# Low part of the MLP weights: an accumulating DMA in place of a VectorE subtraction

## The chip, the cores and the metric

The kernel runs on one core of one Trainium2 chip, and the other cores have no part in it. The metric is the device time of one execution in microseconds. A change is told from no change when the times differ by more than about 2%.

## The reference

One decoder layer in float32 on 512 tokens of 1024 channels: a combined input projection, a recurrent branch and an attention branch, their merge and output projection, then the MLP and a gated per-layer embedding. The change touches the weights of the MLP line alone:

```python
x += (sigmoid(gate_a) * A + sigmoid(gate_b) * B) @ w_out
x += relu(RMSNorm(x) @ w_up)^2 @ w_down          # w_up 1024x4096, w_down 4096x1024
x += (p[l] @ w_ple_proj) * sigmoid(RMSNorm(x) @ w_ple_gate)
```

## The kernel before

All weights lie packed in HBM as 144 units of [128, 1024] float32 (512 KB each), and `weight_order` lists them in order of use. Float32 products are made of three fp32r products: a factor is split into a high part (rounded to fp32r) and a low part (what the rounding left), and `mm3` adds high x high, high x low and low x high. One unit feeds 8 such triples, 24 matmuls of 512 columns, by `proj`.

A unit goes through three steps in `wsplit`. SyncE's queue (SP) loads it into a raw tile `wr`, of which there are two. ScalarE (ACT) copies it into `wh`, which rounds it. VectorE (DVE) subtracts `wh` from `wr` into `wl`. There are four buffers each of `wh` and `wl`. `wload(u)` hands out unit u and first issues the units that follow until four are ready or on their way (`AHEAD = 3`), so the split of unit u+3 is written just ahead of the matmuls of unit u, and it waits until the matmuls of unit u-1 have left their `wh` and `wl`.

The MLP runs in four groups of 1024 hidden channels. A group has 8 up units, each followed by the scaling with `r1`, the squared relu and the split of the result into `us`, and then 8 down units, each of which is added onto `x1`. That makes 64 units, from `U_MLP` = 70 to 133. They follow the 8 units of the output projection (62 to 69), and the per-layer embedding follows them (134 to 143). While the output projection and the last down group run, `sq_accumulate` adds squares on GpSimd (POOL), which has nothing else to do in these stages.

PE, ACT, SP and POOL run their instructions in the order in which the code is written, each engine for itself; a waiting instruction holds up all that stand behind it on its engine. Only VectorE's order is picked by a scheduler.

```python
for c in cuts:
    nc.sync.dma_start(raw[:, c], w_all[u][:, c])
for c in cuts:
    nc.scalar.activation(wh[:, c], raw[:, c], AF.Copy)
    nc.vector.tensor_tensor(out=wl[:, c], in0=raw[:, c], in1=wh[:, c].bitcast(F32),
                            op=ALU.subtract)
```

Of the kernel before, what the change touches and what calls it, by code (L numbers as in the profile page):

```python
# [24 lines left out]

# units of [128, 1024] in the packed weights, in order of use
U_QKV = 0
# [12 lines left out]

# columns of the packed per-channel vectors, 8 each
V_GMIX, V_GMLP, V_GPLE, V_CB, V_BRG, V_BIG, V_LAM, V_CW = 0, 8, 16, 24, 32, 40, 48, 56
N_VEC = 56 + 4 * 8


AHEAD = 3  # weight units split ahead of the one in use
F_BUFS = 24
W_BUFS = 4
N_WARM = 18
CUT = 6  # chunks of a gate projection before the turn of the next queries  # L50
LAG = 2  # chunks between a projection of the recurrent branch and its gates


def weight_order():
    """The units in order of use."""
    def run(u, n=KC):
        return list(range(u, u + n))

    o = run(U_QKV, 12) + run(U_GB) + run(U_GA)
    for m in range(KC + LAG):  # L60
        if m < KC:
            o.append(U_X + m)
        if m >= LAG:
            o.append(U_ATT + m - LAG)
    o += run(U_G) + run(U_RNN) + run(U_OUT) + run(U_MLP, 64) + run(U_PLE, 2) + run(U_PG)
    assert sorted(o + run(U_GATE, 2)) == list(range(N_UNITS))
    return o
# [3 lines left out]
def layer_kernel(ctx, tc, w_all, x_t, p_t, vecs, row, ctab, out_t):  # L71
# [5 lines left out]
    ps = ctx.enter_context(tc.tile_pool(name="ps", bufs=1, space=PSUM))  # L77
    # these engines run their instructions in the order in which they are written here
    E = mybir.EngineType
    ctx.enter_context(tc.manual_schedule(engines={E.PE, E.Activation, E.SP, E.Pool}))  # L80

    def rtile(name):
        """Both parts of four chunks of an activation."""
        return act.tile([P, 4, 2, S], F32R, tag="r", name=name, bufs=4)
# [15 lines left out]

# [1 line left out]
    order = weight_order()  # L102
# [6 lines left out]
    def wsplit(u, pool, bufs, parts=1):  # L109
        raw = wp.tile([P, 1024], F32, tag="wr", name=f"wr{u}", bufs=2)  # L110
        wh = pool.tile([P, 1024], F32R, tag="wh", name=f"wh{u}", bufs=bufs)
        wl = pool.tile([P, 1024], F32R, tag="wl", name=f"wl{u}", bufs=bufs)
        n = 1024 // parts
        cuts = [slice(i * n, (i + 1) * n) for i in range(parts)]
        for c in cuts:
            nc.sync.dma_start(raw[:, c], w_all[u][:, c])
        for c in cuts:
            nc.scalar.activation(wh[:, c], raw[:, c], AF.Copy)  # L118
            nc.vector.tensor_tensor(out=wl[:, c], in0=raw[:, c], in1=wh[:, c].bitcast(F32),  # L119
                                    op=ALU.subtract)  # L120
        return wh, wl

    def wload(u):
        """Unit u, with the units that follow on their way."""
        while u not in ready or (order and len(ready) <= AHEAD):
            wissue()
        return ready.pop(u)

    def split(src, r):
        """r[:, 0] + r[:, 1] = src, both parts exact in 12 bits."""  # L130
        nc.scalar.activation(r[:, 0, :], src, AF.Copy)  # L131
        nc.vector.tensor_tensor(
            out=r[:, 1, :], in0=src, in1=r[:, 0, :].bitcast(F32), op=ALU.subtract
        )

    def split_scaled(src, scale, r):
        """The same for src * scale[partition]."""
        nc.scalar.activation(r[:, 0, :], src, AF.Copy, scale=scale)
        nc.vector.scalar_tensor_tensor(
            out=r[:, 1, :], in0=src, scalar=scale, in1=r[:, 0, :].bitcast(F32),  # L140
            op0=ALU.mult, op1=ALU.subtract,
        )
# [6 lines left out]
    def proj(out, w, acts, ks=range(KC), kcs=KC, w0=0, t=slice(0, S)):  # L149
        """out[c, t] = sum over k of w[k, c] * acts[k, t]."""  # L150
        wh, wl = w
        for k in ks:
            c = slice(w0 + k * P, w0 + (k + 1) * P)
            a = chunk(acts, k)
            mm3(out, wh[:, c], wl[:, c], a[:, 0, t], a[:, 1, t], k == 0, k == kcs - 1)

# [1 line left out]
    vec = const.tile([P, N_VEC], F32, name="vec")  # L158
# [16 lines left out]

# [1 line left out]
    def rms_bcast(sqacc, name):  # L177
        """(mean over channels + eps) ** -0.5 for each token, on every partition."""
        pb = tr_ps(f"pb_{name}")
        nc.tensor.matmul(pb, ones, sqacc, start=True, stop=True)  # L180
        ms = ftile(f"ms_{name}")
        nc.vector.tensor_scalar(out=ms, in0=pb, scalar1=1.0 / D, scalar2=EPS,
                                op0=ALU.mult, op1=ALU.add)
        y = act.tile([P, S], F32, tag="rb", name=f"rb_{name}", bufs=1)
        nc.scalar.activation(y, ms, AF.Abs_reciprocal_sqrt)
        t = ftile(f"nt_{name}")
        nc.vector.tensor_tensor(out=t, in0=y, in1=y, op=ALU.mult)
        nc.vector.tensor_tensor(out=t, in0=t, in1=ms, op=ALU.mult)
        nc.vector.tensor_scalar(out=t, in0=t, scalar1=-0.5, scalar2=1.5,
                                op0=ALU.mult, op1=ALU.add)  # L190
        nc.vector.tensor_tensor(out=y, in0=y, in1=t, op=ALU.mult)
        return y

    def warm_up():
        """Keeps the tensor engine busy, and its clock up, until the first loads are in."""
        pw = tr_ps("pw")
# [8 lines left out]

# [1 line left out]
    xg = rtiles("xg")  # L207
# [13 lines left out]

# [1 line left out]
    att_scope = ExitStack()  # L223
# [4 lines left out]
    def qkv_group(grp, name, after=()):  # L228
        """Projections with tokens on the partitions; after[i]() is emitted behind part i."""
        banks = [mm_ps(f"{name}{n}") for n in range(NB)]  # L230
# [18 lines left out]
    def token_stats():  # L249
        """The mean squares with tokens on the partitions."""  # L250
        ptk = tr_ps("ptk")
# [8 lines left out]

    # rotary tables with the gains folded in: out = t * cc + swap_halves(t) * ss
    def rope_tables(gain, mul, name):
# [21 lines left out]
    def k_side(banks):  # L284
        """Normalized and rotated k of all tokens, v scaled by the norm of its token."""
        kraw = big("kraw")
# [42 lines left out]
    def k_split(kraw, n):  # L329
        # both parts, each doubled, so that a transpose fills all partitions  # L330
        k2 = att.tile([P, 2, 4, 2, HD], F32R, tag="qs", name=f"k2_{n}", bufs=2)
# [29 lines left out]
    def q_scale(u):  # L361
        """(sum of squares over a head + 64 eps mean(x^2)) ** -0.5"""
        n = u % NB
# [144 lines left out]

    # c4 = 4 * softplus(-lambda)
    lam = vec[:, V_LAM : V_LAM + 8]  # L510
# [9 lines left out]
    for d in (15, 13, 11, 9, 7, 5, 3):  # L520
        nc.vector.scalar_tensor_tensor(out=pl, in0=pl, scalar=1.0 / d, in1=s2,
                                       op0=ALU.add, op1=ALU.mult)
    # 4 * log1p(e) = 8 * s * (1 + pl)
    nc.vector.scalar_tensor_tensor(out=pl, in0=pl, scalar=1.0, in1=s_,
# [31 lines left out]

# [1 line left out]
    o = [rtile("o0"), rtile("o1")]  # L558
# [43 lines left out]

# [1 line left out]
    rnn = None  # L604
# [21 lines left out]
    def gate_weights(i):  # L626
        """The gates' weights of two chunks."""
        raw = wp.tile([P, S], F32, tag="wr", name=f"wrg{i}", bufs=2)
# [19 lines left out]
    def gate_post(m, xc, both):  # L648
        r, ig = both
        nc.gpsimd.tensor_tensor(out=ig, in0=ig, in1=xc, op=ALU.mult)  # L650
        # t = tanh(-log_a / 2); a = exp(log_a) = 1 - t (1 + a); sqrt(1 - a^2) = sqrt(t) (1 + a)
        nc.scalar.activation(xc, r, AF.Tanh, scale=cs[:, 0, m : m + 1])
        batch.append((m, r, ig, xc))
# [21 lines left out]
    rnn_scope = ExitStack()  # L675
    later = [[], []]  # what is left of the recurrence, for the next two steps

# [75 lines left out]

# [1 line left out]
    def reload(m):  # L755
# [15 lines left out]

# [1 line left out]
    pr = ple.tile([P, 2, 2, S], F32R, name="pr")  # L773
# [29 lines left out]

# [1 line left out]
    es = []  # L805
# [32 lines left out]

# [1 line left out]
def _units(w):  # L840
    """[1024, 128 n] -> [n, 128, 8 * 128]: unit m holds columns 128 m.., k on the partitions."""
    import numpy as np
# [6 lines left out]
def _pack(i):  # L849
# [30 lines left out]
    row = np.concatenate([i["sinks"][0], i["q_gain"][0], i["k_gain"][0]]).reshape(1, 144)  # L880
    # constants of the shapes: rotary angles and the window's mask
    inv = (10000.0 ** (-np.arange(0, 64, 2) / 64)).astype(np.float32)
# [28 lines left out]
```

## Time and profile before

| | |
|---|---|
| executions timed | 861.26 and 861.58 us, median 861.42 us |
| span of the profiled execution, first to last instruction | 859.3 us |
| PE busy | 851.2 us, 99% of the span |
| DVE busy | 530.6 us, 62% |
| ACT busy | 360.3 us, 42% |
| POOL busy | 113.1 us, 13% |
| granted TensorE clock, mean | 0.999 |

The profiled execution's own time is known by its span: from its first to its last instruction it took 859.3 us, 2.1 us below the median of the timed executions, and these 2.1 us are taken to lie around the first and the last instruction. Busy shares are means over stages with different limits. A matmul's duration in the rows includes its way through the array, and matmuls overlap, so the pace of PE is read from the starts, not from the durations.

### The profile page before, as it was taken

What the parts mean: (1) busy time and instruction counts of PE and PEld (TensorE: products, weight loads), DVE (VectorE), ACT (ScalarE), POOL (GpSimd) and SP (SyncE); (2) the same over time, 40 slices, a digit from 0 to 9 for tenths busy, and PEclk for the clock granted to TensorE, in tenths of its full rate; (3) what the DMA queues carried; (4) which work ended last, traced back from release to release, by engine and by line L of the source; (5) the groups of instructions that cost most, each with busy time, mean ns of one, the idle gap of its engine ahead of it and who ended that gap; (6) DMA issues with size and microseconds to landing.
All of it is one profiled execution on the core that took longest, in us unless ns stands there. A gap on an engine that the chain in (4) does not pass through costs nothing.

```text
span 859.3 us, 10186 instructions
## 1 busy us (share of the span) xinstructions
PE 851.2 (99%) x3922; PEld 698.9 (81%) x3922; DVE 530.6 (62%) x754; ACT 360.3 (42%) x578; POOL 113.1 (13%) x127
## 2 busy tenths in 40 slices
PE   9999999999999999999999999999999999999997
PEld 8878878777788878888888888888888888888886
DVE  4676787778578886776557643564346434655374
ACT  7342656565557787442434221222122212233431
POOL 2811343323111110000120000000000000002100
PEclk9999999999999999999999999999999999999999
DMA  6332212111223222333342332223223222222231
GB/s 238 122 98 74 74 50 74 63 62 50 75 86 110 74 74 94 117 130 127 136 146 84 98 122 93 81 98 102 98 95 98 98 99 98 98 94 93 84 123 50
DMA packets 25536, 83.35 MB, mean 97 GB/s; under 512 B 2960, under 2 KB 3344, under 8 KB 25488
## 3 DMA queue, kind: packets, MB, share of 16 engines
q1 hardware_dynamic: 25344, 82.66, 28.6%
q8 instruction: 31, 0.51, 0.2%
q14 instruction: 17, 0.14, 0.1%
q10 hardware_dynamic: 144, 0.05, 0.0%
HBM read 80.60 MB, written 2.10 MB: 96 GB/s over the span
## 4 chain that ended last, share of the span: by engine, by line
PE 80%; DVE 8%; ACT 6%; DMA 2%; issue 2%; POOL 1%; SPq 0%; ACTq 0%; DVEq 0%; POOLq 0%
PE pu L145 7%; PE pd L147 7%; PE pu L147 7%; PE pd L145 7%; PE pd L146 7%; PE pu L146 7%; PE pgate L145 3%; PE pgate L146 3%; PE pgate L147 3%; DVE xc L619 3%; DVE wl L119 2%; ACT wh L118 2%; PE S L421 2%; PE ppg L147 2%; PE ppg L145 2%; PE ppg L146 2%
## 5 line engine op out<-in xcount | busy, mean ns | idle before, releaser
L119 DVE TENSOR_TENSOR wl<-wr,wh 128x1024 fp32r<-128x1024 f32 (+1 forms) x143 | 179.8, 1258 | 55.9 <-ACT wh L118 55.8
L118 ACT ACTIVATE wh<-wr 128x1024 fp32r<-128x1024 f32 (+1 forms) x143 | 149.0, 1044 | 120.2 <-PE pd L146 96.2
L145 PE MATMUL pu<-x1g,wh 128*128 128x512 f32 x256 | 100.0, 391 | 0.0
L146 PE MATMUL pu<-x1g,wh 128*128 128x512 f32 x256 | 99.6, 389 | 0.0
L147 PE MATMUL pu<-x1g,wl 128*128 128x512 f32 x256 | 99.6, 389 | 0.0
L145 PE MATMUL pd<-u,wh 128*128 128x512 f32 x256 | 99.6, 389 | 0.0
L146 PE MATMUL pd<-u,wh 128*128 128x512 f32 x256 | 99.6, 389 | 0.0
L147 PE MATMUL pd<-u,wl 128*128 128x512 f32 x256 | 99.6, 389 | 0.0
L204 POOL TENSOR_TENSOR sq<-sq,sq_x 128x512 f32<-128x512 f32 x14 | 18.2, 1298 | 456.8 <-ACT sq_x L202 456.8
L131 ACT ACTIVATE u<-up 128x512 fp32r<-128x512 f32 x32 | 20.2, 632 | 126.5 <-DVE up L790 126.5
L799 DVE TENSOR_TENSOR xr<-pd,xr 128x512 f32<-128x512 f32 x32 | 22.1, 692 | 81.4 <-PE pd L147 81.4
L146 PEld LDWEIGHTS pu<-x1g,wh 128*128 128x128 f32 x256 | 48.1, 188 | 10.2 <-issue 0.2
L145 PEld LDWEIGHTS pu<-x1g,wh 128*128 128x128 f32 x256 | 48.1, 188 | 10.1 <-issue 0.2
L147 PEld LDWEIGHTS pu<-x1g,wl 128*128 128x128 f32 x256 | 48.1, 188 | 10.0
L146 PEld LDWEIGHTS pd<-u,wh 128*128 128x128 f32 x256 | 48.1, 188 | 10.0
L147 PEld LDWEIGHTS pd<-u,wl 128*128 128x128 f32 x256 | 48.1, 188 | 10.0
L145 PEld LDWEIGHTS pd<-u,wh 128*128 128x128 f32 x256 | 48.1, 188 | 9.9
L458 POOL TENSOR_SCALAR sm<-sm,st 128x256 f32<-128x256 f32 (+1 forms) x64 | 39.5, 633 | 96.1 <-DVE st L456 57.9
L145 PE MATMUL pgate<-xg,wh 128*128 128x512 f32 x128 | 51.3, 401 | 0.0
L147 PE MATMUL pgate<-xg,wl 128*128 128x512 f32 x128 | 50.1, 391 | 0.0
L146 PE MATMUL pgate<-xg,wh 128*128 128x512 f32 x128 | 50.1, 391 | 0.0
L789 DVE TENSOR_TENSOR up<-pu,rb_x 128x512 f32<-128x512 f32 x32 | 22.1, 691 | 40.0 <-PE pu L147 40.0
(225 smaller groups left out, 1704.6 us busy)
## 6 DMA issues: line engine op xcount, KB each, us to landing
wr<-in_w_all SPq DMA_DIRECT2D x141, 512.0 KB, 3.3
x<-in_x_t SPq DMA_DIRECT2D x8, 256.0 KB, 4.8
xr<-in_x_t SPq DMA_DIRECT2D x8, 256.0 KB, 3.6
out<-pgt SPq DMA_DIRECT2D x7, 256.0 KB, 2.1
wrg<-in_w_all SPq DMA_DIRECT2D x4, 256.0 KB, 2.9
wr<-in_w_all SPq DMA_DIRECT2D x2, 256.0 KB, 3.2
pk<-in_p_t SPq DMA_DIRECT2D x2, 256.0 KB, 3.7
tab<-in_ctab SPq DMA_DIRECT2D x1, 256.0 KB, 6.2
```

The source lines that it names most:

```text
L118: nc.scalar.activation(wh[:, c], raw[:, c], AF.Copy)
L119: nc.vector.tensor_tensor(out=wl[:, c], in0=raw[:, c], in1=wh[:, c].bitcast(F32), op=ALU.subtract)
L131: nc.scalar.activation(r[:, 0, :], src, AF.Copy)
L145: nc.tensor.matmul(out, ah, bh, start=start, stop=False)
L146: nc.tensor.matmul(out, ah, bl, start=False, stop=False)
L147: nc.tensor.matmul(out, al, bh, start=False, stop=stop)
L204: nc.gpsimd.tensor_tensor(out=acc, in0=acc, in1=t, op=ALU.add)
L421: nc.tensor.matmul(pss[:, i, :], q_t[u, g][:, i, :], kt[part][:, kv, b0 * P : b0 * P + 256], start=part == 0, stop=part == 1)
L458: nc.gpsimd.tensor_scalar(out=sm[:, i, :], in0=sm[:, i, :], scalar1=den[:, i : i + 1], scalar2=1.0, op0=ALU.mult, op1=ALU.mult)
L619: nc.vector.scalar_tensor_tensor(out=xc[:, sft:], in0=xb[:, : S - sft], scalar=col(V_CW + 8 * j, m), in1=xc[:, sft:], op0=ALU.mult, op1=AL ...
L789: nc.vector.tensor_tensor(out=y, in0=pu, in1=r1, op=ALU.mult)
L799: nc.vector.tensor_tensor(out=x1[m], in0=pd, in1=x1[m], op=ALU.add)
```

## The change

For the 64 MLP units alone, ACT makes both parts: it copies the raw unit into `wh`, and copies it again with scale -1 into `wl`, which then holds the negated high part. GpSimd's queue then issues a DMA that reads the raw unit and adds it onto `wl` in SBUF, 512 KB onto 512 KB. What is left in `wl` is raw minus high, as before. The subtraction on VectorE is gone for these units. All other units, and the numbers of buffers, stay as they are. The remaining lines of the diff drop comments and shift line numbers by 6.

```diff
         for c in cuts:
             nc.sync.dma_start(raw[:, c], w_all[u][:, c])
+        if U_MLP <= u < U_PLE:
+
+            nc.scalar.activation(wh, raw, AF.Copy)
+            nc.scalar.activation(wl, raw, AF.Copy, scale=-1.0)
+            nc.gpsimd.dma_start(wl, raw, accum_op=ALU.add)
+            return wh, wl
         for c in cuts:
             nc.scalar.activation(wh[:, c], raw[:, c], AF.Copy)
             nc.vector.tensor_tensor(out=wl[:, c], in0=raw[:, c], in1=wh[:, c].bitcast(F32),
```

SP's queue at the turn from the output projection to the MLP, before, with what each instruction waits for (`wr70` is the raw tile of the first MLP unit, `xr` a reloaded chunk of x, `pk` a small input):

```order
L116 DMA wr71_3796<-in_w_all 128x1024 [waits DMAHW0_49,DVE_49]
L757 DMA xr7_3802<-in_x_t 128x512 [waits DMAHW5_49]
L116 DMA wr72_3835<-in_w_all 128x1024 [waits DMAHW2_49,DVE_49]
L776 DMA pk0_3873<-in_p_t 128x512 [waits DMAHW7_49]
L776 DMA pk1_3877<-in_p_t 128x512
L116 DMA wr73_3884<-in_w_all 128x1024 [waits DMAHW4_49,DMAHW1_49,DVE_49]
L116 DMA wr74_3931<-in_w_all 128x1024 [waits DMAHW6_49,DVE_49]
```

The same place of SP's queue with the change (DMASW is the semaphore of a DMA issued by GpSimd):

```order
L116 DMA wr71_3797<-in_w_all 128x1024 [waits DMAHW0_49,DVE_49]
L763 DMA xr7_3804<-in_x_t 128x512 [waits DMAHW5_49]
L116 DMA wr72_3837<-in_w_all 128x1024 [waits DMAHW2_49,DMASW0_49,Activation_49]
L782 DMA pk0_3876<-in_p_t 128x512 [waits DMAHW7_49]
L782 DMA pk1_3880<-in_p_t 128x512
L116 DMA wr73_3887<-in_w_all 128x1024 [waits DMAHW1_49,DMAHW4_49,DMASW1_49,Activation_49]
L116 DMA wr74_3935<-in_w_all 128x1024 [waits DMAHW6_49,DMASW2_49,Activation_49]
```

From unit 72 on, the load into a raw tile waits for the accumulating DMA that read that tile two units earlier, where it waited for VectorE's subtraction; the order itself has not moved.

ACT in the first up group before, where `u0_0` is the split of an up result and `wh74`, `wh75` are high parts:

```order
L131 ACTIVATE u0_0_3882<-up0_0_3926 128x512 [waits DVE_49]
L118 ACTIVATE wh74_3932<-wr74_3931 128x1024 [waits DMAHW2_49,PE_49,Activation_49]
L131 ACTIVATE u0_0_3882<-up0_1_3962 128x512 [waits DVE_49]
L118 ACTIVATE wh75_3968<-wr75_3967 128x1024 [waits DMAHW3_49,PE_49,Activation_49]
L131 ACTIVATE u0_0_3882<-up0_2_3998 128x512 [waits DVE_49]
```

ACT at the same place with the change:

```order
L137 ACTIVATE u0_0_3885<-up0_0_3930 128x512 [waits DVE_49]
L119 ACTIVATE wh74_3936<-wr74_3935 128x1024 [waits DMAHW2_49,PE_49,Activation_49]
L120 ACTIVATE wl74_3937<-wr74_3935 128x1024 [waits DMASW0_49,PE_49]
L137 ACTIVATE u0_0_3885<-up0_1_3967 128x512 [waits DVE_49]
L119 ACTIVATE wh75_3973<-wr75_3972 128x1024 [waits DMAHW3_49,PE_49,Activation_49]
L120 ACTIVATE wl75_3974<-wr75_3972 128x1024 [waits DMASW1_49,PE_49]
L137 ACTIVATE u0_0_3885<-up0_2_4004 128x512 [waits DVE_49]
```

A second copy of 1024 columns stands behind each high part, and it waits for the matmuls and for the accumulating DMA that last used its buffer, four units earlier.

POOL at the turn to the MLP with the change (before, the three `sq1` additions stand in a row, and no DMA is in POOL's queue anywhere):

```order
L121 DMA wl70_3759<-wr70_3757 128x1024 [waits DMAHW2_49,DVE_49,Activation_49]
L210 TENSOR_TENSOR sq1_3563<-sq1_3563,sq_x1_5_3794 128x512 [waits Activation_49,Pool_49]
L121 DMA wl71_3799<-wr71_3797 128x1024 [waits DMAHW4_49,DVE_49,Activation_49]
L210 TENSOR_TENSOR sq1_3563<-sq1_3563,sq_x1_6_3834 128x512 [waits Activation_49,Pool_49]
L121 DMA wl72_3839<-wr72_3837 128x1024 [waits DMAHW6_49,DVE_49,Activation_49]
L210 TENSOR_TENSOR sq1_3563<-sq1_3563,sq_x1_7_3872 128x512 [waits Activation_49,Pool_49]
L121 DMA wl73_3889<-wr73_3887 128x1024 [waits DMAHW1_49,DVE_49,Activation_49]
```

The 64 DMAs are new in POOL's queue, the first few and the last few between additions of squares, the others with nothing between them.

## Rows read from the trace of the kernel before

**Rows 1.** Busy time by stretch: one down group, one up group, the end.

```profile
core 0: us, PE busy (x) PEld busy (x) DVE busy (x) ACT busy (x) POOL busy (x), PEclk, DMA share, GB/s
...
494.00:537.00 43.00, 43.00 (x192) 35.61 (x191) 16.72 (x18) 9.02 (x9) 0.00 (x0) 1.00 0.32 106
537.00:581.00 44.00, 44.00 (x196) 36.45 (x195) 25.02 (x30) 12.14 (x15) 0.00 (x0) 1.00 0.26 88
...
799.00:859.30 60.30, 55.74 (x267) 46.63 (x265) 30.06 (x41) 19.61 (x28) 1.29 (x1) 0.98 0.26 88
```

**Rows 2.** Timeline of PE: first matmul of the MLP and first one behind it.

```profile
449.96 0.39 PE L145 MATMUL pu<-x1g,wh 128*128 128x512 f32 x1
...
799.00 0.39 PE L145 MATMUL pe<-pr,wh 128*128 128x512 f32 x1
```

**Rows 3.** Timeline of ACT in a down group: start, duration, instruction, idle before and releaser.

```profile
592.30 1.06 ACT L118 ACTIVATE wh<-wr 128x1024 fp32r<-128x1024 f32 x1 [4.38 <-PE pd L146]
597.74 1.06 ACT L118 ACTIVATE wh<-wr 128x1024 fp32r<-128x1024 f32 x1 [4.38 <-PE pd L146]
603.13 1.06 ACT L118 ACTIVATE wh<-wr 128x1024 fp32r<-128x1024 f32 x1 [4.33 <-PE pd L146]
```

**Rows 4.** Timeline of DVE and of SP's queue in the same stretch.

```profile
593.39 1.23 DVE L119 TENSOR_TENSOR wl<-wr,wh 128x1024 fp32r<-128x1024 f32 x1 [0.23 <-ACT wh L118]
...
594.65 0.33 SPq L116 DMA_DIRECT2D wr<-in_w_all  x1
```

**Rows 5.** DMA queues and issues: count, KB each, us from issue to landing.

```profile
q1 hardware_dynamic: 25344, 82.66, 28.6%
...
wr<-in_w_all SPq DMA_DIRECT2D x141, 512.0 KB, 3.3
...
out<-pgt SPq DMA_DIRECT2D x7, 256.0 KB, 2.1
...
tab<-in_ctab SPq DMA_DIRECT2D x1, 256.0 KB, 6.2
out<-pgt SPq DMA_DIRECT2D x2, 128.0 KB, 1.7
```

**Rows 6.** Instructions by line and shape from 450 to 800 us: busy us, mean ns, idle before.

```profile
L119 DVE TENSOR_TENSOR wl<-wr,wh 128x1024 fp32r<-128x1024 f32 x64 | 80.2, 1254 | 17.7 <-ACT wh L118 17.7
L118 ACT ACTIVATE wh<-wr 128x1024 fp32r<-128x1024 f32 x64 | 67.3, 1051 | 98.4 <-PE pd L146 96.2 <-issue 2.2
```

**Rows 7.** Waits of SP's queue: total us, times, longest.

```profile
SPq L116 <- DVE wl L119: 562.4, 116, 11.1
```

**Rows 8.** Timeline of POOL at the end of the output projection.

```profile
441.40 1.29 POOL L204 TENSOR_TENSOR sq<-sq,sq_x 128x512 f32<-128x512 f32 x1 [4.15 <-ACT sq_x L202]
446.84 1.29 POOL L204 TENSOR_TENSOR sq<-sq,sq_x 128x512 f32<-128x512 f32 x1 [4.15 <-ACT sq_x L202]
```

## The prediction, made before the run

> **What bounds the kernel now.** I read the busy time by stretch first. The MLP runs from the first `pu` matmul at 449.96 us to the first `pe` matmul behind it at 799.00 us [rows 2], that is 349.0 us for 64 units, 5.45 us a unit. In each of its eight half groups PE is busy for the whole stretch, 43.00 of 43.00 and 44.00 of 44.00 us, at a granted clock of 1.00, with 192 or 196 matmuls [rows 1], one every 0.224 us, or 24 in 5.4 us. So PE sets the MLP's time, and nothing that another engine does faster can shorten it. The only loss of PE in sight lies in the start and the end, where the change is not.
>
> The timelines show how a unit comes to PE. ACT's copies into `wh` come 5.4 us apart, and each has sat idle for 4.3 to 4.4 us until PE was done with an older unit [rows 3]; the buffers of `wh` are what gates it, not the data. In one unit ACT copies from 592.30 to 593.36, DVE subtracts from 593.39 to 594.62, and SP issues the next load into the freed raw tile at 594.65 [rows 3, 4]. SP waits for that subtraction in 116 of its waits, 562.4 us in all [rows 7], which costs nothing so far: the load lands after 3.3 us [rows 5], at 597.95, and ACT reads that tile only at 603.13, two units after 592.30. There are 5.2 us to spare.
>
> **The change part by part.** *Removed:* 64 subtractions of 1.254 us, 80.2 us of DVE [rows 6]. Worth nothing: no half group has PE idle, and DVE is busy for 16.7 us of 43 in a down group and for 25.0 us of 44 in an up group [rows 1].
>
> *Second copy on ACT:* 64 times 1.05 us [rows 6], 67 us. ACT is busy for 9.0 of 43 us in a down group and 12.1 of 44 us in an up group [rows 1]; a unit has 4.3 us of ACT idle ahead of its copy [rows 3], which takes the second one whole. Nothing by itself. What stands behind it on ACT in an up group is the split of the result of the unit that PE has just begun, which is there only 5.4 us later.
>
> *DMAs in POOL's queue:* POOL does nothing in the MLP but the additions of squares, 1.29 us each after 4.15 us of idling [rows 8]. An accumulating DMA waits for ACT's second copy, which stands ahead of that iteration's square on ACT too, so the addition behind it is not held up unless the issue takes over 4 us. Nothing.
>
> *The raw tile's loop:* here the change costs. A raw tile is now free only when the accumulating DMA has landed, and there are two raw tiles. One tile's round is: load 3.3 us [rows 5], two copies of 1.06 us [rows 3], the accumulating DMA from ACT's end to its landing, call it X, and some 0.1 us of handing over (ACT's end to DVE's start was 0.03 us, DVE's end to SP's issue 0.03 us [rows 3, 4]). That is 5.5 + X for two units. PE uses two units in 10.9 us. As long as X is below 5.4 us the loop keeps up, and from there on each us of X makes a unit 0.5 us longer.
>
> The stall does not show at once, since a unit is split three units ahead. Its `wl` is needed 3 x 5.45 = 16.3 us after ACT starts on it and is there after 2.1 + X, so PE has 14.2 - X in hand. 64 loads, those of units 72 to 135, wait for an accumulating DMA. The loss is then 64 x ((5.5 + X)/2 - 5.45) - (14.2 - X) = 33 X - 187 us: nothing below X = 5.7, the 2% (17 us) that a measurement can tell at X = 6.2, and 33 us for each further us.
>
> *X itself* has no row. No accumulating DMA, no DMA from POOL and none from SBUF to SBUF is in this trace. From the nearest rows: all loads together, 82.66 MB, kept 16 engines busy for 28.6% of 859.3 us = 245.8 us [rows 5], which is 336 GB/s or 1.56 us for 512 KB. Of a load's 3.3 us 1.7 us are then delay that does not grow with size. An accumulating DMA must read both tiles and write one. Lower end: it moves like a plain one. Stores of 128 and 256 KB land in 1.7 and 2.1 us [rows 5], so 512 KB would in 2.9 us, and with SP's 0.33 us for an issue [rows 4] X = 3.2 us. Upper end: like the slowest large transfer of the trace, 256 KB in 6.2 us [rows 5], 12.4 us for 512 KB. In between: 1.7 us of delay, twice the 1.56 us since two tiles are read, and about 1.0 us for POOL's issue (between SP's 0.33 us and the 1.29 us of a small POOL instruction [rows 8]), which is 5.8 us. To that comes contention. The two tiles are half a round apart, so the load of one falls into the accumulation of the other, on the same 16 engines; one of them is put off by about the load's 1.56 us. So X = 7.4 us, nearest to the loads' rows, which are of the same size and shape. The engines then work 1.56 + 3.1 = 4.7 us a unit, below 5.45: it is the delay round the loop that binds, not their rate. DMA share in the MLP would go from 0.26 to 0.33 [rows 1] to 0.7 or so.
>
> On the contention the Trainium skill agrees (DMA: Bandwidth & Descriptors, section Issuing engines are not separate DMA queues): transfers run on the same 16 engines and interleave, whichever engine issued them. No row here can show it for POOL.
>
> **The sum.** At X = 7.4 a unit takes (5.5 + 7.4)/2 = 6.45 us, 1.00 us more than now; 64 units make 64 us, less 6.8 us in hand, 57 us. On the profiled execution that is 859.3 + 57 = 916 us of span, and with the 2.1 us around it 918 us; the span with its 2.1 us is the median of 861.4, so it is 57 us above that too, 6.6% slower.
>
> **The rivals.** *The loop keeps up (no change).* If the addition rides along with the stream and the two queues hardly meet, X = 1.7 + 3.1 + 0.33 = 5.1 us, below 5.4: PE stays fully busy, 861 us. For it: 5.2 us to spare and up to 14 us in hand, and four buffers; it decides at X = 5.7, at 6.2 it is still within 2%. Against: any contention with the load's 1.56 us pushes it over. The Trainium skill speaks for it. By its DMA page (DMA: Bandwidth & Descriptors, section Anatomy of one DMA) a DMA issued by GpSimd takes about 2.0 us plus its bytes at 436 GB/s, 3.2 us for 512 KB, which is close to the 3.3 us of SP's load here. Its page Collectives: The Full Stack (section Part 3: Why 7× under link rate) holds that an adding DMA runs at half the rate of a copying one since it reads two sources, and that the add costs nothing; by the two together an estimate of X is 2.0 + 2.4 = 4.4 us, and the time 861 us. No row of this trace shows an adding DMA.
>
> *The DMA engines become the bound.* If adding goes at the upper end, X = 12.4 us, a unit takes 9.0 us and the loss is 222 us, 1084 us. For it: nothing in the trace shows the engines' rate at adding float32, and one transfer was that slow. Against: that one transfer, `tab`, stood behind the loads of x and of the first units in SP's queue, so its time holds theirs too.
>
> *Faster.* It would need PE to get shorter in the MLP; with 43.00 of 43.00 us busy it cannot, unless the matmuls' pace itself depends on what VectorE does beside them. The pace is the same in down groups (192 in 43 us, little DVE) and up groups (196 in 44 us, more DVE) [rows 1], which speaks against it.
>
> **How the numbers follow.** X from 6.2 to 10 us, the loop's loss, 879 to 1004 us: 0.54, with 918 us as its value. The loop keeps up, 861 to 878 us: 0.30. The engines or the addition are slower still, above 1004 us: 0.15. Faster by over 2%: 0.01. The range goes from 861 to 1005 us, which holds the first two and leaves out about 0.17. It is this wide because one unknown, X, is multiplied by 33. The chances: faster 0.01, within 2% 0.30, slower by more 0.69.
>
> **What would show it.** The row of the new DMA's time to landing gives X straight away; below 5.4 us the second case holds. If the loop binds, PE sits idle ahead of the matmuls that read `wl`, released by the DMA, by X/2 - 2.7 us in each unit from about the seventh on; SP's wait is for that DMA; ACT's copies into `wh` wait for the load and no longer for PE; and the stages ahead of 445 us and behind the MLP take what they took. If the engines bind, the DMA share in the MLP is near 1. I would be wrong in the size if the load's 3.3 us grows as well (each us of it counts like one of X), or if the short idle times lower the granted clock: no stretch of this trace has PE idle for a sixth of the time, so no row tells what the clock does then; the end, with PE busy for 55.74 of 60.30 us, still has 0.98 [rows 1].

## The result, and the profile after

The change takes 890.46 us (887.55 and 893.37) against 861.42 us: 29 us more, ratio 1.034, 95% interval 1.032 to 1.036. The execution profiled is the one of 893.37 us, with a span of 891.5 us, so its rows explain 32.2 us of span. I read the stages first: the MLP now runs from 450.19 to 824.21 us, 374.0 us where it took 349.0 [rows 2], 25.0 us more; what stands behind it takes 67.3 us where it took 60.3, 7.0 us more; ahead of it 0.2 us are new. The first matmul of the MLP and the first one behind it:

```profile
450.19 0.39 PE L151 MATMUL pu<-x1g,wh 128*128 128x512 f32 x1
...
824.21 0.39 PE L151 MATMUL pe<-pr,wh 128*128 128x512 f32 x1
```

Busy time by stretch after the change, with the columns of [rows 1]:

```profile
500.00:505.00 5.00, 1.64 (x6) 0.68 (x5) 0.69 (x1) 3.31 (x4) 0.87 (x1) 0.93 0.47 166
505.00:510.00 5.00, 5.00 (x17) 4.03 (x17) 0.69 (x1) 1.10 (x2) 0.87 (x1) 0.73 0.98 184
510.00:550.00 40.00, 40.00 (x178) 33.11 (x178) 4.84 (x7) 14.02 (x14) 5.22 (x6) 1.00 0.76 188
...
830.00:840.00 10.00, 8.49 (x24) 6.46 (x25) 3.90 (x4) 6.27 (x10) 1.27 (x1) 0.66 0.46 157
```

PE is no longer busy throughout: from 500 to 505 us it worked for 1.64 of 5 us. The loss comes in lumps, not in each unit; between the lumps PE runs at its old pace, 178 matmuls in 40 us. Behind a lump the granted clock is low for some microseconds, 0.73 from 505 to 510 us and 0.66 from 830 to 840 us; these are means of stretches in which it stood at its lower level, 1.2 GHz, for a part.

A part of the chain that ended last, in order of time, inside the MLP (start, duration, what):

```profile
503.99 4.57 DMA wl<-wr
...
508.62 4.36 DMA wr<-in_w_all
...
514.04 1.05 ACT wl L120
...
515.38 4.55 DMA wl<-wr
...
519.98 4.40 DMA wr<-in_w_all
```

Here is one full round of a raw tile: the accumulating DMA, the load that waits for it, ACT's two copies, the next accumulating DMA. From 503.99 to 515.38 it takes 11.4 us for two units, where PE needs 10.9. No matmul stands in this part of the chain. It is one of the shorter rounds: the mean of 56 rounds, from unit 76 on, is 11.8 us, made of the load (4.1), the two copies (2.0), 0.3 from ACT's end to POOL's start, the accumulating DMA (5.1) and 0.3 of waiting for ACT and handing over.

The accumulating DMAs go out in pairs, 2.4 and 9.0 us apart, and not half a round apart:

```profile
503.99 0.87 POOL L121 DMA_DIRECT2D wl<-wr  x1 [8.31 <-ACT wl L120]
506.40 0.87 POOL L121 DMA_DIRECT2D wl<-wr  x1 [1.54 <-ACT wl L120]
515.38 0.87 POOL L121 DMA_DIRECT2D wl<-wr  x1 [8.12 <-ACT wl L120]
518.02 0.87 POOL L121 DMA_DIRECT2D wl<-wr  x1 [1.77 <-ACT wl L120]
```

Who waited, in total, times and longest, for PE over the whole span and for SP's queue from 450 to 820 us, and ACT's first copies, with what ended the idle time before them:

```profile
PE pd L151 <- ACT u L137: 9.7, 4, 3.4
PE pu L153 <- DMA wl<-wr: 3.4, 4, 2.8
PE pd L153 <- DMA wl<-wr: 2.6, 3, 1.2
PE pe L151 <- DVE xr L805: 2.0, 1, 2.0
...
SPq L116 <- DMA wl<-wr: 347.5, 63, 10.4
...
L119 ACT ACTIVATE wh<-wr 128x1024 fp32r<-128x1024 f32 x64 | 67.6, 1056 | 207.1 <-DMA wr<-in_w_all 200.2
```

SP's loads wait for the accumulating DMA where they waited for VectorE [rows 7]. ACT's copies into `wh` wait for the load for 200.2 of 207.1 us, where they waited for PE [rows 6]: the loop sets their start, no longer the buffers of `wh`. PE's largest waits are not for `wl` but for the split of an up result, four times, once at each turn from up to down units.

DMA queues and issues of the profiled execution from 500 to 790 us, and the accumulating DMA's instructions on POOL (duration ns min/median/max, first and last start):

```profile
q0 software_dynamic: 7118, 25.95, 50.0%
q1 hardware_dynamic: 7144, 25.99, 25.4%
...
wl<-wr POOLq DMA_DIRECT2D x50, 512.0 KB, 5.0
wr<-in_w_all SPq DMA_DIRECT2D x49, 512.0 KB, 4.3
...
L121 POOL DMA_DIRECT2D wl<-wr x64: 869/869/1060, 438.2 to 812.0; - x64
```

The accumulating DMA lands after 5.0 us, and for the same bytes it holds the engines twice as long as a load (50.0% against 25.4%). Loads land after 4.3 us instead of 3.3 [rows 5]. The last row gives the pace: 63 steps from 438.2 to 812.0 us, 5.93 us a unit, where PE could do with 5.45.

### The profile page after: what moved, and what is told of

Same layout as the page of the kernel before. It is cut to its first block, busy times and chain, and to the rows that moved or that the text cites. A ratio compares the mean times of both kernels' runs of the same rounds, so it can differ in the third digit from the quotient of the medians.

```text
span 891.5 us, 10324 instructions
## 1 busy us (share of the span) xinstructions
PE 862.2 (97%) x3922; PEld 701.4 (79%) x3922; DVE 448.6 (50%) x690; ACT 420.0 (47%) x642; POOL 169.1 (19%) x191
## 4 chain that ended last, share of the span: by engine, by line
PE 46%; DMA 28%; DVE 9%; issue 8%; ACT 8%; POOL 1%; POOLq 0%; ACTq 0%; SPq 0%; DVEq 0%
DMA wr<-in_w_all 15%; DMA wl<-wr 13%; PE pgate L151 3%; PE pgate L152 3%; PE pgate L153 3%; DVE xc L625 3%; DVE wl L125 3%; ACT wh L124 2%; PE S L427 2%; PE ppg L153 2%; PE ppg L151 2%; PE ppg L152 2%; PE pya L151 2%; PE pout L153 2%; PE pya L153 2%
## 5 line engine op out<-in xcount | busy, mean ns | idle before, releaser
L119 ACT ACTIVATE wh<-wr 128x1024 fp32r<-128x1024 f32 x64 | 67.6, 1056 | 207.1 <-DMA wr<-in_w_all 200.2
L125 DVE TENSOR_TENSOR wl<-wr,wh 128x1024 fp32r<-128x1024 f32 (+1 forms) x79 | 99.2, 1258 | 44.9 <-ACT wh L124 44.7
L121 POOL DMA_DIRECT2D wl<-wr x64 | 56.0, 875 | 304.1 <-ACT wl L120 251.7
L151 PE MATMUL pd<-u,wh 128*128 128x512 f32 x256 | 101.0, 394 | 9.7 <-ACT u L137 9.7
L152 PE MATMUL pd<-u,wh 128*128 128x512 f32 x256 | 100.7, 393 | 0.7 <-DVE u L138 0.7
L124 ACT ACTIVATE wh<-wr 128x1024 fp32r<-128x1024 f32 (+1 forms) x79 | 81.8, 1039 | 28.4 <-DMA wr<-in_w_all 16.3
L138 DVE TENSOR_TENSOR u<-up,u 128x512 fp32r<-128x512 f32 x32 | 22.2, 692 | 109.2 <-ACT u L137 109.1
L120 ACT ACTIVATE wl<-wr 128x1024 fp32r<-128x1024 f32 x64 | 66.7, 1043 | 0.0
L151 PEld LDWEIGHTS pd<-u,wh 128*128 128x128 f32 x256 | 48.4, 189 | 21.2 <-ACT u L137 11.4
L151 PE MATMUL pgate<-xg,wh 128*128 128x512 f32 x128 | 51.3, 401 | 0.0
```

The lines of the kernel that those rows point to most:

```text
L119: nc.scalar.activation(wh, raw, AF.Copy)
L120: nc.scalar.activation(wl, raw, AF.Copy, scale=-1.0)
L121: nc.gpsimd.dma_start(wl, raw, accum_op=ALU.add)
L138: nc.vector.tensor_tensor(out=r[:, 1, :], in0=src, in1=r[:, 0, :].bitcast(F32), op=ALU.subtract)
L151: nc.tensor.matmul(out, ah, bh, start=start, stop=False)
L152: nc.tensor.matmul(out, ah, bl, start=False, stop=False)
```

## The experiments

The theory: two raw tiles, each tied up by load, copies and accumulating DMA for longer than PE needs for two units. The rivals: the share of the 16 DMA engines sets the pace; ACT's second copy does; each accumulating DMA has a fixed price. "Before" is the kernel before, run on the same chip, 860.8 to 861.4 us in the four groups of runs; a run is compared with the kernel before of its own group.

**A third raw tile.**

```diff
+        if U_MLP <= u < U_PLE:
+            raw = ple.tile([P, 1024], F32, tag="wr3", name=f"wr{u}", bufs=3)
+        else:
             raw = wp.tile([P, 1024], F32, tag="wr", name=f"wr{u}", bufs=2)
```

> The MLP units get three raw tiles of their own in place of two; all else as in the change. The round theory (two raw tiles, each tied up for 11.4 us by load, two copies and the accumulating DMA, so 5.7 us a unit where PE needs 5.45): three tiles allow 3.8 us a unit, PE stays fully busy in the MLP, 861 us with some 3 us either way. The engine theory (loads and accumulations share 16 engines at a DMA share of 0.75 and that sets the pace): a third tile adds no rate, 885 us or more. The ACT theory (the second copy and its place in ACT's queue cost the time): ACT's work is the same, 885 to 892 us.

861.7 us, ratio 1.001 (1.000 to 1.002): the whole loss is gone. DMA issues of this run from 500 to 780 us, and its busy time by stretch (columns of [rows 1]; the share of the DMA engines is the last but one):

```profile
wr<-in_w_all SPq DMA_DIRECT2D x53, 512.0 KB, 4.9
wl<-wr POOLq DMA_DIRECT2D x51, 512.0 KB, 6.0
...
500.00:780.00 280.00, 280.00 (x1237) 231.83 (x1236) 72.00 (x104) 119.99 (x135) 47.67 (x54) 1.00 0.85 196
```

Both DMAs are slower here than in the change, 4.9 and 6.0 us to landing, and nothing is lost. The engines are busy for 0.85 of the stretch, in the change for 0.76, so their share was not the bound.

**VectorE adds instead of the DMA.**

```diff
-            nc.gpsimd.dma_start(wl, raw, accum_op=ALU.add)
+            nc.vector.tensor_tensor(out=wl, in0=raw, in1=wl.bitcast(F32), op=ALU.add)
```

> ACT makes both copies as in the change, but VectorE adds the raw unit onto the negated part instead of the DMA. The round theory and the engine theory: a raw tile is tied up for 3.3 + 2.1 + 1.25 = 6.7 us of 10.9, so nothing is lost, 861 us within 2 us. The ACT theory: the second copy is still there, 885 to 892 us.

860.85 us, ratio 1.000 (0.999 to 1.001). ACT's second copy is still there, and costs nothing by itself.

**A plain DMA in place of the adding one.**

```diff
-            nc.gpsimd.dma_start(wl, raw, accum_op=ALU.add)
+            nc.gpsimd.dma_start(wl, raw)
```

> The DMA from GpSimd stays, but copies the raw unit onto wl instead of adding it: the low part then holds the raw weights. If the second read is what makes the DMA long (1.56 us by the loads' rate), its landing falls from 5.0 to 3.4 us, the round to 9.9 us, and the time to 861 to 866 us. If the length is that of any DMA that GpSimd issues, the landing stays at about 5 us and the time at 885 to 892 us.

861.72 us, ratio 1.001 (1.000 to 1.002). This kernel leaves out the subtraction of the high part and is read for its time alone. Its DMA queues and issues from 500 to 780 us:

```profile
q1 hardware_dynamic: 7415, 26.97, 28.5%
q0 software_dynamic: 7488, 27.27, 27.4%
...
wr<-in_w_all SPq DMA_DIRECT2D x52, 512.0 KB, 3.3
wl<-wr POOLq DMA_DIRECT2D x51, 512.0 KB, 3.0
```

A plain DMA from GpSimd's queue lands in 3.0 us, its issue included. Adding costs 2.0 us more at the medians, or 1.55 us against the 4.55 us of the rounds shown above, and the loads beside the plain DMA stay at 3.3 us. It also takes the engines as long as a load of the same size, not twice as long: what adding adds is about a second pass of 512 KB.

**The up results' high part by VectorE**, so that no split stands behind a weight copy on ACT.

```diff
-            split(y, chunk(us, m))
+            r = chunk(us, m)
+            nc.vector.tensor_copy(r[:, 0, :], y)
+            nc.vector.tensor_tensor(out=r[:, 1, :], in0=y, in1=r[:, 0, :].bitcast(F32),
+                                    op=ALU.subtract)
```

> As the change, but the high part of each up result is copied by VectorE instead of ACT, so that on ACT nothing of the activations stands behind a weight copy that waits for its load. If ACT's order is what turns the slow round into idle time of PE at the four turns from up to down units (9.7 us of waits for the split, and the low clock behind them), these go and the time falls to 872 to 880 us. If the round's rate alone makes the loss, 887 to 892 us.

892.87 us, ratio 1.035 (1.032 to 1.039), as slow as the change. PE's waits in this run:

```profile
PE pu L153 <- DMA wl<-wr: 12.9, 14, 2.1
PE pd L153 <- DMA wl<-wr: 11.2, 14, 1.7
```

The 9.7 us of waits for the split are gone and 24.1 us of waits for `wl` have come instead. ACT's order decides only where PE stands still. The theory that it made the loss falls. The mean granted clock of this execution, the slowest of the four (898.38 us), is 1.000, so the loss does not need a low clock either.

**Each unit in two halves.**

```diff
-            nc.scalar.activation(wh, raw, AF.Copy)
-            nc.scalar.activation(wl, raw, AF.Copy, scale=-1.0)
-            nc.gpsimd.dma_start(wl, raw, accum_op=ALU.add)
+            for c in (slice(0, 512), slice(512, 1024)):
+                nc.scalar.activation(wh[:, c], raw[:, c], AF.Copy)
+                nc.scalar.activation(wl[:, c], raw[:, c], AF.Copy, scale=-1.0)
+                nc.gpsimd.dma_start(wl[:, c], raw[:, c], accum_op=ALU.add)
```

> As the change, but each unit is cut in two halves of 512 columns: copy, negated copy and accumulating DMA of the first half, then of the second, so that the first half is being added while ACT copies the second. The amount of work is the same, with twice as many DMAs of 256 KB. The round theory: the first DMA starts 1.0 us earlier, the round falls from 11.4 us to some 10.4 us, below PE's 10.9 us, and the time to 861 to 868 us. If the DMA engines' share sets the pace, nothing falls, 885 us or more.

895.76 us, the median of the three of its four executions that lie within 0.2% of each other (the fourth took 909.38 us), ratio 1.041 (1.039 to 1.043): missed, it got slower. From its chain of work, its timeline of POOL, PE's largest wait, and busy time by stretch:

```profile
573.86 0.87 POOL wl L122
...
574.89 3.81 DMA wl<-wr
...
578.84 5.44 DMA wr<-in_w_all
...
577.09 0.87 POOL L122 DMA_DIRECT2D wl<-wr  x1 [1.33 <-ACT wl L121]
578.13 0.87 POOL L122 DMA_DIRECT2D wl<-wr  x1 [0.17 <-issue]
...
PE pd L152 <- ACT u L138: 19.8, 4, 5.6
...
500.00:512.00 12.00, 8.37 (x25) 6.39 (x25) 1.38 (x2) 4.89 (x9) 3.48 (x4) 0.72 0.79 177
```

POOL takes 0.87 us for half a unit as for a whole one, so the second half is issued 1.03 us after the first; ACT's first copy started at 572.40 us, and the tile is free at 578.70, after 6.3 us, 0.7 us earlier than with whole units (2.1 + 0.3 + 4.55 us). But that holds for every other unit only. The next unit's second half goes out at 578.13 us, lands only at 584.11 us, beside the load that the first unit had released, and keeps its tile for 8.5 us; that load takes 5.4 us. Over 56 rounds a tile is tied up by copies and DMAs for 7.5 us on the mean (7.4 with whole units), the load takes 4.25 us (4.1), and the round 12.0 us (11.8): cutting the units gained nothing in the round. What else differs from the change is how PE waits: at the four turns for 19.8 us in place of 9.7, and the granted clock is 0.72 over 12 us at each of them, 0.983 over the span in place of 0.992. That this makes the kernel slower than the change, and why the DMAs of a pair stretch each other, no run here shows.

**The first 16 and the first 32 units alone.**

```diff
-        if U_MLP <= u < U_PLE:
+        if U_MLP <= u < U_MLP + 16:
```

> The change for the first 16 MLP units alone (70 to 85), the others by VectorE as before. The round theory: a unit costs PE 0.4 to 0.5 us more than it has (the 64 DMAs went out 5.93 us apart on average, PE needs 5.45), so 16 units fall behind by 6 to 8 us, which the 9 us in hand cover: 861 to 863 us. If each accumulating DMA costs its part at once, a quarter of 30 us: 868 us.

> The change for the first 32 MLP units (70 to 101). The round theory: 32 units fall behind by 13 to 16 us, of which 9 are in hand, 864 to 870 us. If each accumulating DMA costs its part at once, half of 30 us: 876 us.

869.07 and 875.99 us, ratios 1.010 (1.008 to 1.013) and 1.019 (1.015 to 1.022): 8.2 and 15.1 us, a quarter and half of the 29 us. (Both are below 2%, but their intervals leave out 1.000.) By both expectations the fixed price wins here; the 9 us in hand did not show. The cause stands at the start of the MLP in the change's timeline of ACT:

```profile
456.26 1.06 ACT L119 ACTIVATE wh<-wr 128x1024 fp32r<-128x1024 f32 x1 [2.86 <-DMA wr<-in_w_all]
...
464.80 0.63 ACT L137 ACTIVATE u<-up 128x512 fp32r<-128x512 f32 x1 [4.59 <-DVE up L796]
465.34 1.04 ACT L119 ACTIVATE wh<-wr 128x1024 fp32r<-128x1024 f32 x1
```

ACT waits for the first up result, which waits for the norm `r1`, and the next weight copy stands behind it: it starts at 465.34 us, when PE has been done with the buffer since 456.1 us and its load, issued at 454.65 us, has landed since 459.0 us. That is 6.4 us late, and it spends the lead of three units: this unit (74) has its low part at 472.18 us, and PE starts on it at 472.82. In the kernel before the same wait is there (its copy starts at 463.78 us), but a raw tile is tied up for only 5.7 us there (3.3 + 1.06 + 1.25 + 0.1), which makes it good.

**One more copy on ACT**, which moves nothing by DMA.

```diff
             nc.scalar.activation(wh, raw, AF.Copy)
+            spare = ple.tile([P, 1024], F32, tag="spare", name=f"spare{u}", bufs=1)
+            nc.scalar.activation(spare, raw, AF.Copy)
             nc.scalar.activation(wl, raw, AF.Copy, scale=-1.0)
```

> As the change, with one more copy of the raw unit on ACT, into a spare tile that nobody reads, between the two copies; it moves nothing by DMA. The round theory: the raw tile is tied up for 1.0 us longer, half of that a unit, 64 units: 32 us more than the change, 915 to 928 us. If the DMA engines' share sets the pace, ACT has the time to spare (some 3.5 us busy of 5.9 a unit): 885 to 895 us.

933.79 us, ratio 1.085 (1.082 to 1.088), 43 us above the change, somewhat over the 25 to 38 expected. ACT's spare copies give the pace:

```profile
L121 ACT ACTIVATE spare<-wr x64: 1038/1042/1047, 438.4 to 853.5; 128x1024 f32<-128x1024 f32 x64
```

It is 6.59 us a unit, 0.66 us more than in the change for 1.0 us in the round, where 0.5 was expected. The mean round is 13.1 us, 1.3 more than in the change: the copy, and some 0.3 us more of waiting for ACT.

**The copies in the other order**, the DMA issued between them.

```diff
-            nc.scalar.activation(wh, raw, AF.Copy)
             nc.scalar.activation(wl, raw, AF.Copy, scale=-1.0)
             nc.gpsimd.dma_start(wl, raw, accum_op=ALU.add)
+            nc.scalar.activation(wh, raw, AF.Copy)
```

> As the change, with ACT's two copies in the other order: the negated copy first, the DMA issued behind it, and the copy into the high part while the DMA runs. The same work, the same DMAs. The round theory: the raw tile is tied up for 1.0 us less, the pace falls from 5.93 us a unit by 0.5 us to PE's 5.45 us, 861 to 867 us. If the number and size of the DMAs set the loss, 885 to 893 us.

861.87 us, ratio 1.000 (0.999 to 1.001). Its issues from 500 to 780 us and its DMAs on POOL:

```profile
wr<-in_w_all SPq DMA_DIRECT2D x52, 512.0 KB, 4.1
wl<-wr POOLq DMA_DIRECT2D x51, 512.0 KB, 5.0
...
L120 POOL DMA_DIRECT2D wl<-wr x64: 857/869/1055, 437.2 to 784.4; - x64
```

The DMAs are the same in number, size and length to landing as in the change, and the loads too within 0.2 us; only the second copy now runs beside the DMA. The pace is 5.51 us, the mean round 10.9 us, and the MLP takes 349.0 us as before. With the run with one more copy this shows the round from both sides. It also settles the fixed price: the same 64 accumulating DMAs cost nothing here.

**Sixteen later units, and all units from the second group on.** The condition of the change is `U_MLP + 16 <= u < U_MLP + 32`, then `U_MLP + 16 <= u < U_PLE`.

> The change for 16 units of the second MLP group alone (86 to 101) in place of the first 16 (70 to 85), which cost 8.2 us. The theory that the time in hand was already spent at the start of the MLP, where ACT waits for the first up results ahead of the next weight copies: in the second group some 9 us are in hand, the 16 units fall behind by 8 us, and the time is 861 to 864 us. The theory that each accumulating DMA costs 0.5 us at once wherever it stands: 869 us.

> The change for the units from the second MLP group on (86 to 133, 48 of 64). With some 9 us in hand at its start: 48 x 0.48 = 23 us less 9, 875 us (872 to 878). With nothing in hand: 884 us (881 to 886).

865.57 us, ratio 1.004 (1.002 to 1.005): 4.2 us for the medians, half of what the first 16 units cost, between the two expectations. The pace was the same as theirs (5.97 and 5.99 us):

```profile
L121 POOL DMA_DIRECT2D wl<-wr x16: 869/869/1057, 524.2 to 614.0; - x16
```

So 16 units fell behind by 16 x 0.54 = 8.6 us and some 4 us of it were in hand, not 9. The theory of a fixed price wherever a DMA stands, 869 us, falls with this run too. The 48 units took 890.68 us, ratio 1.032 (1.028 to 1.036), above both expectations; the profiled execution of this kernel, 883.37 us, is the fastest of its four, the others lie at 890.61 to 891.98. Its pace is 5.97 us, which makes 48 x 0.52 = 25 us, and it lost 22. The three slower ones lost some 30 us, as much as the change with 64 units, which neither theory explains. What they did differently no profile shows; the slowest has the highest mean clock of the four, 0.998, so it is not the clock.

## Why the prediction was right, and what was off

The forecast was 57 us more, 918 us, with 861 to 1005; measured were 29 us more, 890 us. Direction and mechanism were right, the size was twice too large, and 7 of the 32 us of the profiled execution lie behind the MLP, where the sum had nothing.

**What bounds and what is worth nothing.** Right. Removing 80 us of VectorE work gained nothing, and the second copy on ACT by itself cost nothing (860.85 us with VectorE adding). POOL's additions of squares were not held up either.

**The raw tile's loop.** Right, and shown: a third tile, a shorter DMA and an earlier DMA each bring 861 to 862 us back, and a longer round costs 43 us more. These four runs carry the claim. Set beside the pace of the accumulating DMAs, the losses are:

| kernel | units | pace, us | units x (pace - 5.45) | MLP longer, profiled execution | measured over before |
|---|---|---|---|---|---|
| the change | 64 | 5.93 | 31 | 25.0 | 29 |
| first 16 | 16 | 5.97 | 8 | 6.0 | 8.2 |
| first 32 | 32 | 5.96 | 16 | 12.5 | 15.1 |
| one more copy | 64 | 6.59 | 73 | 66.7 | 72.9 |
| later 16 | 16 | 5.99 | 9 | 4.0 | 4.2 |
| later 48 | 48 | 5.97 | 25 | 19.6 | 29 (22.0 in the profiled execution) |

The agreement by itself is no test of the cause: PE and the DMAs go through the same units, so whatever holds up PE shows in this pace too. The fourth column is 2 to 6 us above the fifth, which is the lead that was in hand; that the sixth agrees with the fourth where the units start the MLP is in part chance, since it holds losses outside the MLP as well (7.0 us behind it in the change).

**X, the mis-sized term.** I put X, from ACT's end to the landing, at 7.4 us; it measured 0.3 + 5.0 = 5.3 us at the medians. That is below the 5.4 us that I had named as the sign of a loop that keeps up, so by that sign alone there would be no loss. What tips the round is the load, 0.8 us longer on the mean (4.1 in place of 3.3) and 1.0 at the medians; I had named that as a way to be wrong in the size, and had put the whole contention into X. The two together stand for 6.2 us of X by the means (5.4 and 0.8), where the forecast had 1.2 more. Two of its four terms held. The second read was put at 1.56 us and measured 1.55 to 2.0. The contention was put at 1.56 us and measured 1.0 us on the load (3.3 to 4.3) and 0.45 us on the accumulating DMA (4.55 to 5.0), though not in the way I had it: the DMAs of the two tiles go out 2.4 us apart, so an accumulating DMA runs beside the other tile's one and the load that follows that. What was too large is the delay that does not grow with size together with POOL's issue, 1.7 + 1.0 = 2.7 us: the plain DMA from GpSimd's queue landed in 3.0 us with its issue, which leaves 1.4 us, and another 0.3 us lie between ACT's end and POOL's start. One microsecond too many in X is 33 us by my own formula.

**The time in hand.** I counted 6.8 us. It was there, but the start of the MLP spends it, since ACT waits there for `r1`'s first result: the DMAs of units 72 and 74 went out 18.5 us apart, where PE takes 10.9. That wait was in the trace of before, and I had left it out. From unit 74 on the DMAs went out 5.84 us apart, and 60 units at 0.39 us are 23 us, near the 25.0 us by which the MLP grew. So this error went the other way and took some 7 us off the first.

**ACT's order.** I said that nothing on PE's path stands behind the second copy. At the four turns something does: the last up result's split waits behind a weight copy that waits for its load, and PE waited 9.7 us for it. At the first turn, after the change:

```profile
501.69 1.06 ACT L119 ACTIVATE wh<-wr 128x1024 fp32r<-128x1024 f32 x1 [6.66 <-DMA wr<-in_w_all]
...
503.60 0.61 ACT L137 ACTIVATE u<-up 128x512 fp32r<-128x512 f32 x1
```

The run with VectorE's copy shows that this only moves the loss, so the sum did not need it; but PE's waits were not found where I had said, ahead of each matmul that reads `wl`.

**The end and the clock.** I expected the stages behind the MLP to take what they took; they took 7.0 us more, with 3.0 us of waits in the embedding and a low clock around 835 us. The clock was named as a risk without a row; it did fall after two of the lumps in the MLP, which by the rows of 1 us each cost about 1.7 us apiece, and the mean over the span is 0.992 instead of 0.999. Of the MLP's 25.0 us the waits of PE listed above make some 16; for about 5 no row was found.

**The rivals.** The loop that keeps up missed by 0.9 us a round: 11.8 us on the mean against 10.9. The estimate of 4.4 us for X from the Trainium skill (DMA: Bandwidth & Descriptors, section Anatomy of one DMA, with Collectives: The Full Stack, section Part 3) is close to the 4.55 us that the DMA took in the rounds shown. The Trainium skill's statement, on the second of these pages, that an add needs two source reads agrees with the 1.55 to 2.0 us here. What the estimate leaves out, 0.3 us ahead of the issue, the 0.45 us on the DMA and the 0.8 to 1.0 us on the load beside it, decided the case. The engines as a bound are refuted by the third tile, a fixed price of each DMA by the copies in the other order.

**Open.** How much is in hand in the middle of the MLP (4 to 5 us by the two runs that start there), why three executions of the kernel with 48 units took 7 to 9 us more than the profiled one, as much as with all 64, and why the stages behind the MLP wait at all.

## What to carry to other kernels

Ask of a moved operation not only whether its engine has time, but which buffer it holds and for how long: add up the round of that buffer, load and all, divide by the number of buffers, and compare with the time the bounding engine needs for as many tiles. What the round is too long by, divided by the number of buffers, is lost in every step; a lead of a few tiles pays for it only where no other wait has spent the lead. Here one more buffer or one overlapped step in the round was the remedy. Count in the round what its transfers do to each other: a lengthening of the load beside the new DMA counts as much as the new DMA's own length. Taking away the wait that the profile names can leave the loss as it is, if that wait is only where a slow loop comes to light.

## What the runs showed of the hardware that was not expected

GpSimd was busy for 0.87 us for an accumulating DMA of 256 KB as for one of 512 KB on the same 128 partitions, and for 0.54 us for a plain one of 512 KB. A plain DMA from SBUF to SBUF that it issued landed in 3.0 us, sooner than the 3.3 us of a load from HBM issued by SP. In the change, after PE had idled for 3.4 us in one piece (to 504.26 us), the granted clock stood at its lower level of 1.2 GHz, and was back at 2.4 GHz from 508 us on:

```profile
505.00:506.00 1.00, 1.00 (x3) 0.82 (x3) 0.00 (x0) 1.00 (x2) 0.00 (x0) 0.50 0.68 131
506.00:507.00 1.00, 1.00 (x4) 0.79 (x3) 0.69 (x1) 0.10 (x1) 0.60 (x1) 0.50 1.03 197
507.00:508.00 1.00, 1.00 (x5) 0.77 (x4) 0.00 (x0) 0.00 (x0) 0.27 (x1) 0.63 1.06 197
508.00:509.00 1.00, 1.00 (x6) 0.83 (x5) 0.00 (x0) 0.00 (x0) 0.00 (x0) 1.00 1.05 197
```

After waits of 2.0 and 1.05 us in the embedding it was 0.50 from 832 to 838 us. In the run with the up results' high part on VectorE PE waited for `wl` 28 times in the MLP, for up to 2.1 us each, and the clock stayed at 1.00 throughout the MLP.
